# FFN stages of a two-layer trunk: down products moved inside the gate/up blocks, smaller chunks, layer vectors loaded at another place

## The chip, the cores and the metric

The kernel runs on one core of one Trainium2 chip. The metric is the device time of one execution in microseconds (us). Below, TensorE (PE in the profile, with PEld for its weight loads) does the matrix products, VectorE (DVE) and ScalarE (ACT) the elementwise work, GpSimd (POOL) and SyncE (SP) issue transfers (DMAs). SBUF is the working memory, PSUM the memory that matmuls write, here in banks of 512 float32 a partition.

## The reference

The input is 512 tokens of 1024 float32 features; 16 learned tokens are put in front, so T = 528. Two layers follow, each with two feed-forward networks (FFN) around a mixer:

```python
def _swiglu(x, wg, wu, wd):
    return (jax.nn.silu(x @ wg) * (x @ wu)) @ wd

for l in range(DEPTH):                       # DEPTH = 2
    h = _layer_norm(ALPHA * h + 0.5 * _swiglu(h, ffn1_wg[l], ffn1_wu[l], ffn1_wd[l]), ln1_g[l], ln1_b[l])
    m = _mixer(h, ...)                       # convolution branch and RWKV-7 branch
    h = _layer_norm(ALPHA * h + m, ln2_g[l], ln2_b[l])
    h = _layer_norm(ALPHA * h + 0.5 * _swiglu(h, ffn2_wg[l], ffn2_wu[l], ffn2_wd[l]), ln3_g[l], ln3_b[l])
```

wg and wu are 1024 x 2816, wd is 2816 x 1024. The change touches the four FFNs and the loading of the small per-layer vectors, and nothing of the mixer.

## The kernel before

**Products in three parts.** Every float32 operand is held as a high part, rounded to the type float32r, and a low part, the remainder. A product is three matmuls for each 128 rows of the contraction: high x high, high x low, low x high (`mac1`, L204 to L214; the matmul is L210). Features lie on the 128 partitions, tokens along the free dimension, in two halves of n = 264 (256 in the last FFN, which leaves out the 16 learned tokens). KT = 8 is the number of 128-row pieces of the model width, FT = 22 that of the FFN's inner width.

**Splitting weights.** `wunit` (L122) loads a 128 x 1024 piece of weights (512 KB) on SP's queue into a tile `w_raw`, copies it to `w_hi` on ScalarE (L142) and subtracts on VectorE to get `w_lo` (L153). `halve` (L113) does the same for parts of a block; with `dma` set it puts the negated raw weights into `w_lo` on ScalarE (L117) and lets GpSimd issue a DMA that adds the raw weights there (L118), without it VectorE subtracts (L120). The split weights lie in entries of a ring (`entry`, L108), which in an FFN has eight: two, two and four from three pools.

**One FFN** (`ffn`, L427). The inner width is worked off in chunks of 8, 8 and 6 of the 22 pieces (`CHUNKS`, L26). For each chunk come first its gate/up blocks, one for each piece of 128 inner features, and then eight down products, one for each 128 output features, which add their part to `y`. Inner activations are held split, in `hh` and `hl`, eight pieces at a time.

- The first four pieces (`PLAIN`, L27) are *plain* (`up`, L443): gate and up product for each half of the tokens, 2 x 2 x 8 x 3 = 96 matmuls. Then ScalarE's Silu (L457), VectorE's product (L458) and the split into `hh` and `hl` (L105, L106).
- The other 18 are blocks of *seven products* (`up7`, L463), the Strassen-Winograd way for a 2 x 2 cut of weights and tokens: 7 x 4 x 3 = 84 matmuls instead of 96. Their loads (L470) bring gate and up weights (512 KB each) into raw tiles, two from each of two pools by turns. VectorE forms four sums of halves (L476), and five parts are split, three of them through GpSimd's adding DMA. The products go into four banks a, b, c, d of PSUM in the order w1 to a, w6 to b, w7 to c, w5 to d, w2 to a, q4 to c, w3 to d; the last three add to what stands in the bank. Between them VectorE takes the banks' contents over into the tile `ln_sq` (L499), so q4 must wait until c's first content has been read, and w3 the same for d. Two closings (L513) and splits (L105, L106) end a block.
- `make_seven` (L524) builds the token sums t1 to t4 that these blocks use: VectorE first adds high and low part of all tokens into `y` (L534), then forms sums and splits them. t1 overwrites a quarter of the token tile, so it stands behind the last plain block.
- A down product (`down`, L558) loads one piece of wd for the chunk's rows, splits it, and runs 8 (in the last chunk 6) x 3 matmuls for each half; VectorE adds the bank to `y` (L571 for the first chunk, L574 later). For the last chunk it also adds up `ssum` over the features (`add_sum`, L425).

PSUM has six banks for these products (`mm`, L437) and two for the norms' sums. `ln_sq` has two buffers, `w_raw` two in either pool.

**Order.** `stream` (L165) runs the jobs one after another: load and split, products, evacuation. The framework's scheduler then puts each engine's instructions into a fixed order, near that of the program, and may draw loads forward where a buffer is free by its own account; on the chip each engine and queue works in that order, and each instruction waits there for what it needs. The last three jobs (`TAIL`, L41), three downs, are run half by half: all three for the first half of tokens, then the weights ahead for the next stage (`fetch_ahead`, L663) and the first part of the first half's norm (`layer_norm`, L372: mean matmul L380, subtraction L385, square L387, sums L395 to L398, variance matmul L400, reciprocal L402), then all three for the second half. The rest of the norm is run under the start of the next stage.

**Layer vectors.** `layer_vectors` (L313) loads sixteen vectors and time_mix into parts of the tile `ssum` (L321, L323) and conv_w into a tile from the FFN's `ln_sq` buffers (L324), and turns them with TensorE (L327, L328, L336). Both layers' calls are jobs of the very first FFN (L1593), put into the job list at places 4 and 8.

Of the kernel before, what the change touches and what calls it, by code (L numbers as in the profile page):

```python
# [7 lines left out]
F32 = mybir.dt.float32  # L8
# [8 lines left out]
P = 128  # L17
D = 1024
KT = D // P
# [6 lines left out]
CHUNKS = ((0, 8), (8, 16), (16, FT))  # L26
PLAIN = 4  # L27
# [64 lines left out]
class Trunk:  # L92
# [220 lines left out]
    def layer_vectors(self, l, room, mm):  # L313
# [10 lines left out]
        nc.sync.dma_start(out=cwn, in_=self.d["conv_w"][l])  # L324
        vec = lp.tile([P, P], F32, name="vec")
# [101 lines left out]
    def ffn(self, l, which, t0, n, gname, bname, pre, final=False, head=None, extra=()):  # L427
# [7 lines left out]
        tok = [slice(t0 + h * n, t0 + (h + 1) * n) for h in range(2)]  # L435

# [6 lines left out]
        def up(fc, f):  # L443
            cs = slice(fc * P, (fc + 1) * P)

            def load():
                return self.wunit(wg[:, :, cs]), self.wunit(wu[:, :, cs])

            def mac(w, h):
                ps = mm(), mm()  # L450
                return ps, [self.mac1(ps[i][:, :n], w[i], self.x, tok[h], KT) for i in range(2)]

            def evac(h, ps):
                if h == 0:
                    held[fc] = fp.tile([P, 4, 264], F32, name="ln_sq", bufs=2)
                g = held[fc][:, h, :n]
                nc.scalar.activation(g, ps[0][:, :n], AF.Silu)  # L457
                nc.vector.tensor_tensor(g, g, ps[1][:, :n], op=ALU.mult)  # L458
                self.split(g, hh[:, f, tok[h]], hl[:, f, tok[h]])

            return load, mac, evac

        def up7(fc, f):  # L463
            cs = slice(fc * P, (fc + 1) * P)

            def load():
                pool = (self.wp, fp)[fc % 2]
                raw = [pool.tile([P, KT, P], F32, name="w_raw", bufs=2) for _ in range(2)]
                for r, w in zip(raw, (wg, wu)):
                    nc.sync.dma_start(out=r, in_=w[:, :, cs])  # L470
                g1, g2, u1, u2 = (r[:, k:k + KH] for r in raw for k in (0, KH))
                sums = fp.tile([P, 3 * KH, P], F32, name="sums", bufs=1)
                s1 = fp.tile([P, KH, P], F32, name="sum1", bufs=2)
                s2, s3, s4 = (sums[:, i * KH:(i + 1) * KH] for i in range(3))
                for o, a, b in ((s1, u1, u2), (s3, g1, u1), (s2, s1, g1), (s4, s2, g2)):
                    nc.vector.tensor_tensor(o, a, b, op=ALU.add)  # L476
                his, los = zip(*(self.entry() for _ in range(4)))
                lower = slice(0, KH)
                upper = slice(KH, KT)
                whole = slice(0, KT)  # L480
                parts = ((0, whole, raw[0], True), (2, lower, s1, True), (2, upper, u2, True),
                         (1, whole, sums[:, :KT], False), (3, lower, s4, False))
                for e, k, src, dma in parts:
                    self.halve(src, his[e][:, k], los[e][:, k], dma)
                block = lambda e, k: (his[e][:, k], los[e][:, k])
                return [block(0, lower), block(1, lower), block(1, upper), block(2, lower),
                        block(0, upper), block(2, upper), block(3, lower)]

            def mac(w, h):
                if h:  # L490
                    return None, [()]
                w1, w6, w7, w5, w2, q4, w3 = w
                x11, x21, x22, t1, t2, t3, t4 = seven
                run = lambda ps, w, x, first, last: self.together([
                    self.mac1(ps[:, :n], w, x[:2], x[2], KH, x[3], first, last, True)])
                a, b, c, d = (mm() for _ in range(4))
                z = fp.tile([P, 4, 264], F32, name="ln_sq", bufs=2)
                e0, e1, e2, e3 = (z[:, i, :n] for i in range(4))
                add = lambda o, x, y: nc.vector.tensor_tensor(o, x, y[:, :n], op=ALU.add)  # L499
                run(a, w1, x11, True, True)  # L500
                nc.scalar.copy(e0, a[:, :n])
                run(b, w6, t2, True, True)
                add(e0, e0, b)
                run(c, w7, t3, True, True)
                add(e1, e0, c)
                run(d, w5, t1, True, True)
                add(e1, e1, d)
                run(a, w2, x21, False, True)
                nc.scalar.activation(e3, a[:, :n], AF.Silu)
                run(c, q4, t4, False, True)  # L510
                add(e2, e0, c)
                out = [(hh[:, f, t], hl[:, f, t]) for t in tok]
                close = lambda u, g, h: (nc.vector.scalar_tensor_tensor(  # L513
                    u, u, -1.0, g, op0=ALU.mult, op1=ALU.mult), self.split(u, *out[h]))
                close(e2, e3, 0)
                run(d, w3, x22, False, True)
                add(e0, e0, d)
                nc.scalar.activation(e0, e0, AF.Silu)
# [1124 lines left out]
```

## Time and profile before

| | |
|---|---|
| median of 3 runs | 3206.27 us (3200.68 to 3208.75) |
| the profiled execution | 3209.99 us |
| its span, first to last instruction | 3208.3 us |
| mean granted TensorE clock | 0.964 |
| 0 to 447 us | first FFN, with the layer vectors and its norm |
| 447 to 1244 us | mixer of the first layer |
| 1244 to 1646 us | second FFN |
| 1646 to 2046 us | third FFN |
| 2046 to 2816 us | mixer of the second layer |
| 2816 to 3208 us | fourth FFN, norm and store |

The profile is of one execution. Its page gives busy time by engine and the transfers by issuing line with their median time from issue to landing. A view by stretches gives, for each stretch of time, the busy time of each engine and in brackets its number of instructions, then the clock that TensorE was granted (1.00 is full), the mean busy share of the 16 DMA engines and GB/s. Matmuls overlap, so a busy TensorE isn't TensorE at its peak; the count of matmuls in a stretch says more. The view of groups has, behind the bar, busy us and mean ns of one, and behind the second bar the idle time of the engine just before the group, with what ended it. In a timeline a row has start and duration in us, the engine and line, output and input, and in brackets the idle time before it and what ended it. `DVE ln_sq L499` is VectorE's instruction of line 499 that writes `ln_sq`.

### The profile page before, as it was taken

Reading aid. Unit: us, or ns where it says so; the run is one execution under the profiler, and the core shown is the slowest. Engines: PE = TensorE matmul, PEld = TensorE weight load, DVE = VectorE, ACT = ScalarE, POOL = GpSimd, SP = SyncE. Lnnn points to the kernel's source line nnn. Section 1 sums busy time; section 2 is a strip of 40 time slices with the busy share of each in tenths; the row PEclk is TensorE's granted clock in tenths of the full one; section 3 lists DMA queues with packets and bytes.
Section 4 is the critical chain, followed back from the end, with each engine's and each line's share of the span. In section 5 each row is a group of like instructions: output and inputs, shape, how many; then the busy total and the mean of one; then the engine's idle time right before and its main releaser. Section 6 shows DMA issues by size and latency. Waiting matters only on the chain.

```text
span 3208.3 us, 64745 instructions
## 1 busy us (share of the span) xinstructions
PE 3022.6 (94%) x26308; PEld 2878.5 (90%) x26308; DVE 2177.7 (68%) x4471; ACT 1496.6 (47%) x2649; POOL 239.4 (7%) x358
## 2 busy tenths in 40 slices
PE   6999989999999899999989999899999999999997
PEld 5999989989888799999989999899888889989997
DVE  5554667888886677654685646778887748675655
ACT  4453545343554444453554534543444446264543
POOL 1010100000000000010101200000000000011110
PEclk8999999998999999999999999999999999999998
DMA  6566535334455544675636755343353556455761
GB/s 162 129 148 146 120 98 179 97 86 108 119 125 130 174 145 96 147 150 141 152 91 153 165 127 131 123 152 98 89 128 94 140 127 187 120 131 139 180 137 59
DMA packets 607032, 418.77 MB, mean 131 GB/s; under 512 B 90444, under 2 KB 542400, under 8 KB 606734
## 3 DMA queue, kind: packets, MB, share of 16 engines
q1 hardware_dynamic: 564910, 308.49, 33.9%
q0 software_dynamic: 37216, 97.62, 17.3%
q10 hardware_dynamic: 4608, 8.52, 0.7%
q8 instruction: 207, 3.39, 0.4%
q14 instruction: 91, 0.75, 0.1%
HBM read 270.81 MB, written 47.12 MB: 99 GB/s over the span
## 4 chain that ended last, share of the span: by engine, by line
PE 65%; DMA 12%; DVE 9%; issue 9%; ACT 4%; POOL 1%; SPq 0%; ACTq 0%; POOLq 0%; DVEq 0%
PE mm L210 34%; PE mm L229 17%; DMA w_raw<-in_ffn_wu_dram 4%; DMA w_raw<-in_ffn_wd_dram 3%; DMA w_lo<-w_raw 3%; DVE w_lo L153 2%; PE sc L1236 2%; ACT w_hi L142 1%; PE sc L1155 1%; PE tr L1305 1%; PE ch L1330 1%; PE tr L1313 1%; PE ch L1322 1%; POOL w_lo L118 1%; DMA a<-ascr 1%
## 5 line engine op out<-in xcount | busy, mean ns | idle before, releaser
L210 PE MATMUL mm<-xh,w_hi 128*128 128x264 f32 (+1 forms) x1728 | 501.7, 291 | 48.8 <-DVE ln_sq L499 22.6
L210 PE MATMUL mm<-xl,w_hi 128*128 128x264 f32 (+1 forms) x1728 | 499.9, 290 | 0.4
L210 PE MATMUL mm<-xh,w_lo 128*128 128x264 f32 (+1 forms) x1728 | 498.4, 289 | 0.0
L142 ACT CAST w_hi<-w_raw 128x1024 fp32r<-128x1024 f32 (+1 forms) x224 | 227.8, 1018 | 430.7 <-PE mm L210 157.6
L153 DVE TENSOR_TENSOR w_lo<-w_raw,w_hi 128x1024 fp32r<-128x1024 f32 (+2 forms) x280 | 303.5, 1084 | 157.6 <-ACT w_hi L142 151.0
L210 PE MATMUL mm<-hh,w_hi 128*128 128x264 f32 (+1 forms) x1408 | 401.3, 285 | 6.7 <-ACT hh L105 6.6
L210 PE MATMUL mm<-hl,w_hi 128*128 128x264 f32 (+1 forms) x1408 | 400.2, 284 | 2.5 <-DVE hl L106 1.3
L229 PE MATMUL mm<-xh,w_hi 128*128 128x264 f32 x1760 | 393.5, 300 | 7.6 <-DVE kp L858 2.9
L210 PE MATMUL mm<-hh,w_lo 128*128 128x264 f32 (+1 forms) x1408 | 399.1, 283 | 0.0
L229 PE MATMUL mm<-xh,w_lo 128*128 128x264 f32 x1760 | 392.6, 299 | 4.6 <-DMA w_lo<-w_raw 3.3
L229 PE MATMUL mm<-xl,w_hi 128*128 128x264 f32 x1760 | 392.8, 298 | 0.0
L210 PEld LDWEIGHTS mm<-xh,w_hi 128*128 128x128 f32 x1728 | 334.1, 194 | 55.7 <-DVE ln_sq L499 25.1
L984 DVE SCALAR_TENSOR_TENSOR cacc<-cu,cw,cacc 128x528 f32<-128x528 f32 (+1 forms) x480 | 355.6, 752 | 3.4
L210 PEld LDWEIGHTS mm<-xl,w_hi 128*128 128x128 f32 x1728 | 335.7, 194 | 1.8 <-DVE xl L417 1.6
L210 PEld LDWEIGHTS mm<-xh,w_lo 128*128 128x128 f32 x1728 | 335.6, 194 | 0.1
L229 PEld LDWEIGHTS mm<-xh,w_hi 128*128 128x128 f32 x1760 | 287.4, 195 | 16.0 <-DVE kp L858 3.2
L229 PEld LDWEIGHTS mm<-xh,w_lo 128*128 128x128 f32 x1760 | 286.4, 195 | 12.3 <-DMA w_lo<-w_raw 4.1
L229 PEld LDWEIGHTS mm<-xl,w_hi 128*128 128x128 f32 x1760 | 286.5, 194 | 7.6 <-issue 0.2
L210 PEld LDWEIGHTS mm<-hh,w_hi 128*128 128x128 f32 x1408 | 264.9, 188 | 9.7 <-ACT hh L105 9.4
L210 PEld LDWEIGHTS mm<-hl,w_hi 128*128 128x128 f32 x1408 | 265.1, 188 | 6.2 <-DVE hl L106 6.1
L210 PEld LDWEIGHTS mm<-hh,w_lo 128*128 128x128 f32 x1408 | 265.3, 188 | 0.0
L118 POOL DMA_DIRECT2D w_lo<-w_raw x144 | 124.3, 864 | 1319.9 <-ACT w_lo L117 658.4
(356 smaller groups left out, 6715.7 us busy)
## 6 DMA issues: line engine op xcount, KB each, us to landing
w_raw<-in_w_in_dram SPq DMA_DIRECT2D x116, 512.0 KB
w_lo<-w_raw POOLq DMA_DIRECT2D x104, 512.0 KB, 4.9
w_raw<-in_ffn_wg_dram SPq DMA_DIRECT2D x88, 512.0 KB
w_raw<-in_ffn_wu_dram SPq DMA_DIRECT2D x88, 512.0 KB
w_raw<-in_ffn_wd_dram SPq DMA_DIRECT2D x64, 512.0 KB
w_lo<-sum POOLq DMA_DIRECT2D x72, 256.0 KB, 3.9
w_lo<-w_raw POOLq DMA_DIRECT2D x72, 256.0 KB, 5.2
w_raw<-in_ffn_wd_dram SPq DMA_DIRECT2D x32, 384.0 KB
```

Source lines behind the costliest of these rows:

```text
L118: self.nc.gpsimd.dma_start(out=lo.bitcast(F32), in_=x, accum_op=ALU.add)
L142: copy = self.nc.scalar.copy(hi[:, :kt], raw[:, :kt])
L153: sub = self.nc.vector.tensor_tensor(lo[:, k], raw[:, k], hi[:, k].bitcast(F32), op=ALU.subtract)
L210: self.nc.tensor.matmul(pm, a[:, k, :], b[:, xk + k, s], start=first and k == 0 and j == 0, stop=last and k == nk - 1 and j == 2, skip_gro ...
L229: m = nc.tensor.matmul(pm[:, h, :n], a[:, wk + k, :], b[:, xk + k, s:s + n], start=first and k == 0 and j == 0, stop=last and k == nk - 1 ...
L984: tap = nc.vector.scalar_tensor_tensor(y, x, w, y, op0=ALU.mult, op1=ALU.add)
L1155: pairs.append(nc.tensor.matmul(ps[:, e, p * P:(p + 1) * P], FB[p][r, fs], G[r, p, 1, :, cs], start=True, stop=True))
L1236: nc.tensor.matmul(ps[r, i, cs], vt[r, i], x[r, i, cs], start=True, stop=True)
L1305: nc.tensor.matmul(tr[0:C, right(h)], G[:, h // 2, h % 2, 0, cs], sv[:, h, :], start=True, stop=True)
L1313: chain.append(nc.tensor.matmul(tr[C:P, right(h)], G[0:C, h // 2, h % 2, 1, cs], w[0:C, h, :], start=True, stop=True))
L1322: nc.tensor.matmul(ch[HS:P, left(h)], SB[:, c, h, C:2 * C], va[:, h, :], start=True, stop=True, skip_group_check=True)
L1330: chain.append(nc.tensor.matmul(ch[0:C, right(h)], SB[:, c, h, 0:C], va[:, h, :], start=False, stop=True, skip_group_check=True))
```

## The change

- The chunks are of 4, 4, 4, 4, 2 and 4 pieces, and there are five plain blocks instead of four.
- A block of seven products calls `between` behind its fifth product; the order is now w1, w6, w7, w2, w5, then `between`, then q4 and w3. `between` runs one or two *pairs* of down products of the preceding chunk. A pair is two neighbouring outputs: one load of 256 columns (512 KB for four pieces), one split into one entry of the ring, then two products for each half of 4 x 3 matmuls (2 x 3 for the chunk of two pieces), each added to `y`. In the chunk of two pieces two pairs stand in each block. A plain block runs its pair behind its own products.
- The last chunk's eight downs stand behind everything. Their four pairs of weights are prepared ahead; all eight run for the first half, then come `fetch_ahead` and the start of the norm, then all eight for the second half.
- Raw tiles turn over in a fixed order through five buffers, two of the weights' pool and three of the FFN's, for the loads of gate, up and pairs alike (and for the first layer tokens and conv_w). s1 is split by VectorE and not through GpSimd's adding DMA, so two of five parts go that way. The four sums share one tile.
- `y` gets the first half's tokens by two GpSimd DMAs (high part, then low part added) instead of VectorE additions; the token sums are begun behind the third block, and t1 is made behind the fifth.
- The layer vectors' loads are issued behind one block and the transposes behind the next: the first layer's behind the third and fourth block, the second layer's behind the fifth and sixth. conv_w goes to a raw tile.

The core of the diff:

```diff
-CHUNKS = ((0, 8), (8, 16), (16, FT))
-PLAIN = 4
+CHUNKS = ((0, 4), (4, 8), (8, 12), (12, 16), (16, 18), (18, FT))
+PLAIN = 5
...
         nc.sync.dma_start(out=cwn, in_=self.d["conv_w"][l])
+        yield True
         vec = lp.tile([P, P], F32, name="vec")
...
+        def raw():
+            i = raws[0] % 5
+            raws[0] += 1
+            return fp.tile([P, KT, P], F32, name="w_raw", bufs=3) if i > 1 else self.wp.tile(
+                [P, KT, P], F32, name="w_raw", bufs=WB[0])
...
+        def load7(f):
+            cs = slice(f * P, (f + 1) * P)
+            g, u = raw(), raw()
...
+            sums = fp.tile([P, 4, KH, P], F32, name="sums", bufs=1)
...
+            for e, k, src, dma in ((0, whole, g, True), (1, whole, sv[:, :KT], False),
+                                   (2, lower, s1, False), (2, upper, u2, True),
+                                   (3, lower, s4, False)):
+                self.halve(src, his[e][:, k], los[e][:, k], dma)
...
+        def up7(f, between):
+            w1, w6, w7, w5, w2, q4, w3 = load7(f)
...
+            run(a, w1, x11, True, True)
+            nc.scalar.copy(e0, a[:, :n])
+            run(b, w6, t2, True, True)
+            add(e0, e0, b)
+            run(c, w7, t3, True, True)
+            add(e1, e0, c)
+            run(a, w2, x21, False, True)
+            nc.scalar.activation(e3, a[:, :n], AF.Silu)
+            run(d, w5, t1, True, True)
+            add(e1, e1, d)
+            between()
+            run(c, q4, t4, False, True)
+            add(e2, e0, c)
+            close(e2, e3, 0)
+            run(d, w3, x22, False, True)
...
+        def load_pair(a, b, o):
+            hi, lo = self.entry()
+            k = 2 * (b - a)
+            r = raw()[:, :k]
+            nc.sync.dma_start(out=r.rearrange("p (k o) c -> p k (o c)", o=2),
+                              in_=wd[:, a:b, o * P:(o + 2) * P])
+            self.split(r, hi[:, :k], lo[:, :k])
+            return [(hi[:, i:k:2], lo[:, i:k:2]) for i in range(2)]
...
+        def pair(a, b, o):
+            ws = load_pair(a, b, o)
+            for i, w in enumerate(ws):
+                for h in range(2):
+                    pd, products = down(a, b, o + i, w, h)
+                    self.together(products)
+                    add_down(a, b, o + i, h, pd)
...
+        for part, kw in zip(self.x, ({}, {"accum_op": ALU.add})):
+            nc.gpsimd.dma_start(out=y[:, :, tok[0]], in_=part[:, :, tok[0]].bitcast(F32), **kw)
...
+        def later(f):
+            if f == m:
+                join_x(1)
+                next(sums)
+            if f == PLAIN - 1:
+                next(sums)
+            for x in extra[:1]:
+                if next(x, None) is None:
+                    extra.pop(0)
+
+        for i, (a, b) in enumerate(CHUNKS):
+            pairs = [(*CHUNKS[i - 1], o) for o in range(0, KT, 2)] if i else []
+            share = -(-len(pairs) // (b - a))
+
+            def between():
+                for _ in range(min(share, len(pairs))):
+                    pair(*pairs.pop(0))
...
-        self.stream(jobs[m:], TAIL, before,
-                    lambda: self.fetch_ahead(l, which), lambda: next(first))
+        a, b = CHUNKS[-1]
+        if which == 1:
+            self.ring(*self.wy)
+        ws = [w for o in range(0, KT, 2) for w in load_pair(a, b, o)]
+        for h in range(2):
+            if h == 1:
+                self.fetch_ahead(l, which)
+                next(first)
+            for o in range(KT):
...
+                    pd, products = down(a, b, o, ws[o], h)
+                    self.together(products)
+                add_down(a, b, o, h, pd)
```

More of the change, by code (lines that the diff above doesn't have):

```diff
@@ L441, in st @@
             return mm("st", 2)
[L443 to L518, printed above, removed]
-                close(e1, e0, 1)
-                return None, [()]
-            return load, mac, lambda h, ps: None
@@ L580, in ffn @@
-        jobs, held, seven = [], {}, []
-        for a, b in CHUNKS:
-            jobs += [(up if f < PLAIN else up7)(f, f - a) for f in range(a, b)]
-            jobs += [down(a, b, o) for o in range(KT)]
-        sums = make_seven()
-        for i in (PLAIN, PLAIN - 1):
-            jobs.insert(i, (lambda: next(sums), lambda w, h: (None, [()]), lambda h, ps: None))
-        for i, f in extra:
-            jobs.insert(i, (lambda f=f: f(mm), lambda w, h: (None, [()]), lambda h, ps: None))
-        fpool = fp = y = ssum = hh = hl = None
@@ L596, in room @@
             hh, hl = (fp.tile([P, KT, T], F32R, name=x) for x in ("hh", "hl"))
[L597 to L598 removed]
+            return y, ssum, lambda: raw().rearrange("p k c -> p (k c)")
+        def raw():
[3 more added lines that the diff above has]
+                [P, KT, P], F32, name="w_raw", bufs=WB[0])
@@ new lines, in scratch, with inner, load, plain @@
+        def scratch():
+            return fp.tile([P, 4, 264], F32, name="ln_sq", bufs=2)
+        def inner(f, h):
+            return hh[:, f % KT, tok[h]], hl[:, f % KT, tok[h]]
+        def load(f):
+            cs = slice(f * P, (f + 1) * P)
+            return self.wunit(wg[:, :, cs]), self.wunit(wu[:, :, cs])
+        def plain(w, h):
+            ps = mm(), mm()
+            return ps, [self.mac1(ps[i][:, :n], w[i], self.x, tok[h], KT) for i in range(2)]
+        def gate(f, h, ps, z):
+            g = z[:, h, :n]
+            nc.scalar.activation(g, ps[0][:, :n], AF.Silu)
+            nc.vector.tensor_tensor(g, g, ps[1][:, :n], op=ALU.mult)
+            self.split(g, *inner(f, h))
@@ new lines, in up7, with close @@
+        def up7(f, between):
+            w1, w6, w7, w5, w2, q4, w3 = load7(f)
+            x11, x21, x22, t1, t2, t3, t4 = seven
+            run = lambda ps, w, x, first, last: self.together([
+                self.mac1(ps[:, :n], w, x[:2], x[2], KH, x[3], first, last, True)])
+            a, b, c, d = (mm() for _ in range(4))
+            z = scratch()
+            e0, e1, e2, e3 = (z[:, i, :n] for i in range(4))
+            add = lambda o, x, y: nc.vector.tensor_tensor(o, x, y[:, :n], op=ALU.add)
+            def close(u, g, h):
+                nc.vector.scalar_tensor_tensor(u, u, -1.0, g, op0=ALU.mult, op1=ALU.mult)
+                self.split(u, *inner(f, h))
+            run(a, w1, x11, True, True)
[13 more added lines that the diff above has]
+            run(d, w3, x22, False, True)
+            add(e0, e0, d)
+            nc.scalar.activation(e0, e0, AF.Silu)
+            close(e1, e0, 1)
@@ L600, in ffn @@
+        seven = []
         if head is not None:
@@ L605, in ffn @@
         ws = self.ahead
-        ws += [load() for load, mac, evac in jobs[len(ws):m]]
+        ws += [load(f) for f in range(len(ws), m)]
         self.ahead = []
         def heads(h):
-            ps, products = zip(*(jobs[j][1](ws[j], h) for j in range(m)))
+            ps, products = zip(*(plain(ws[f], h) for f in range(m)))
             self.together([x for xs in products for x in xs])
```

144 lines of the change are left out of this document (85 added, 59 removed).

## The prediction

> **What bounds the kernel now.** I read the page, then the stretches by stage, then the groups with their idle time, then timelines inside the feed-forward (FFN) stages. The page:
>
> ```profile
> span 3208.3 us, 64745 instructions
> PE 3022.6 (94%) x26308; PEld 2878.5 (90%) x26308; DVE 2177.7 (68%) x4471; ACT 1496.6 (47%) x2649; POOL 239.4 (7%) x358
> w_lo<-w_raw POOLq DMA_DIRECT2D x104, 512.0 KB, 4.9
> w_lo<-sum POOLq DMA_DIRECT2D x72, 256.0 KB, 3.9
> ```
>
> TensorE is the bound; the question is where it stands still or runs slowly. The stretches by stage (times, matmul counts in brackets, granted clock, DMA share):
>
> ```profile
> core 0: us, PE busy (x) PEld busy (x) DVE busy (x) ACT busy (x) POOL busy (x), PEclk, DMA share, GB/s
> 54.20:77.20 23.00, 0.23 (x3) 0.15 (x2) 10.24 (x17) 4.89 (x10) 2.57 (x3) 0.58 0.58 138
> 77.20:95.00 17.80, 17.80 (x133) 17.74 (x134) 5.70 (x9) 4.92 (x9) 0.00 (x0) 0.87 0.01 2
> 95.00:419.00 324.00, 312.21 (x2509) 308.72 (x2509) 180.41 (x342) 147.52 (x246) 41.28 (x48) 0.99 0.61 141
> 130.00:200.00 70.00, 69.62 (x570) 69.21 (x570) 33.68 (x60) 28.30 (x44) 8.59 (x10) 1.00 0.52 121
> 200.00:240.00 40.00, 34.06 (x266) 32.99 (x265) 25.25 (x49) 24.35 (x44) 9.49 (x11) 0.98 0.87 191
> 234.90:237.90 3.00, 0.27 (x4) 0.05 (x2) 1.10 (x3) 2.19 (x4) 1.22 (x2) 1.00 0.90 181
> 237.90:241.90 4.00, 4.00 (x21) 4.00 (x22) 3.25 (x7) 1.34 (x3) 0.51 (x1) 0.60 1.01 146
> 419.00:447.00 28.00, 19.12 (x128) 17.63 (x127) 25.80 (x43) 13.05 (x20) 0.00 (x0) 0.88 0.15 39
> 1282.00:1615.00 333.00, 316.56 (x2520) 312.86 (x2521) 195.95 (x355) 154.01 (x254) 41.22 (x48) 0.98 0.63 146
> 1340.00:1385.00 45.00, 45.00 (x372) 45.00 (x371) 17.40 (x32) 13.22 (x19) 5.17 (x6) 1.00 0.48 106
> 1385.00:1480.00 95.00, 89.05 (x693) 87.37 (x692) 60.80 (x115) 54.45 (x94) 15.46 (x18) 0.96 0.76 172
> 1646.00:2003.00 357.00, 346.10 (x2796) 342.71 (x2795) 213.84 (x388) 176.65 (x291) 46.43 (x54) 1.00 0.62 139
> 2850.00:3174.00 324.00, 306.44 (x2531) 302.94 (x2530) 185.62 (x348) 148.81 (x252) 43.01 (x50) 0.98 0.63 141
> 3150.00:3170.00 20.00, 20.00 (x170) 20.00 (x171) 7.61 (x18) 0.00 (x0) 0.00 (x0) 1.00 0.01 2
> ```
>
> At 1340 to 1385, pure down products, TensorE never waits: 45/372 = 0.121 us a matmul, my yardstick (0.1176 in the last FFN, 20/170). Against it:
>
> - 54.2 to 95: 40.8 us for 136 matmuls worth 16.5: **24.3 us** lost.
> - The four FFN bodies: 324 - 2509 x 0.121 = 20.4; 333 - 2520 x 0.121 = 28.1; 357 - 2796 x 0.121 = 18.7; 324 - 2531 x 0.1176 = 26.4. Together **93.6 us**.
>
> Inside a body the loss isn't spread evenly. Down products at 130 to 200 lose 70 - 69.0 = 1.0 us at a DMA share of 0.52; blocks of seven products at 200 to 240 lose 40 - 32.2 = 7.8 at 0.87, and 1385 to 1480, which is mostly blocks, 11.1 of 95. What the blocks wait for, from the groups and the VectorE and TensorE timelines:
>
> ```profile
> L476 DVE TENSOR_TENSOR sum<-w_raw 128x512 f32<-128x512 f32 x72 | 49.7, 691 | 164.8 <-DMA w_raw<-in_ffn_wu_dram 164.8
> ```
> ```profile
> 205.30 0.69 DVE L476 TENSOR_TENSOR sum<-w_raw 128x512 f32<-128x512 f32 x1 [7.58 <-DMA w_raw<-in_ffn_wu_dram]
> 205.91 0.42 DVE L499 TENSOR_TENSOR ln_sq<-ln_sq,mm 128x264 f32<-128x264 f32 x1
> 211.44 0.42 DVE L499 TENSOR_TENSOR ln_sq<-ln_sq,mm 128x264 f32<-128x264 f32 x1
> ```
> ```profile
> 211.91 0.39 PE L210 MATMUL mm<-t4h,w_hi 128*128 128x264 f32 x1 [1.69 <-DVE ln_sq L499]
> ```
>
> VectorE runs in order. The sum of the next block's raw weights stands ahead of this block's evacuations (L499); it waits 7.58 us for a load, the evacuations fall behind, and q4, which goes on in bank c, waits 1.69 us for c's earlier evacuation. So the loads are late, VectorE passes the lateness on, and TensorE pays.
>
> **The change, part by part.** *Layer vectors.* Gap and its cause:
>
> ```profile
> L336 PE MATMUL mm<-ident,ln_sq 31*128 31x31 f32 x8 | 1.0, 287 | 22.8 <-DMA ln_sq<-in_conv_w_dram 22.8
> ```
> ```profile
> 54.69 0.48 SPq L321 DMA_DIRECT2D ssum<-in_ln_g_dram  x1
> 63.62 0.57 SPq L323 DMA_DIRECT2D ssum<-in_time_mix_dram  x1
> 69.78 24.88 SPq L324 DMA_DIRECT2D ln_sq<-in_conv_w_dram  x2
> ```
>
> The transposes of conv_w stand in TensorE's queue 22.8 us before their data: conv_w's load needs a ln_sq buffer (two, which the gates and token sums share) and is issued only at 69.78. Changed, conv_w has its own raw buffer (the free second and third of the three in the FFN's pool), and a block stands between the loads and the transposes: 96 matmuls, 11.6 us, plus hoisting. I take all 24.3 us back. The second layer's loads still hold SP's queue for some 9 us (54.69 to 63.62), weight loads behind them; a block with its pair (16.0 us, below) covers that. If it doesn't, at most those 9 us return, so 15 to 24.
>
> *Downs inside the blocks.* A unit is now 84 + 48 = 132 matmuls, 16.0 us. Three raw tiles of five turn over in it: each has 5/3 x 16.0 = 26.6 us from load to load, against 2 x 84 x 0.121 = 20.3 in a run of blocks now. Split weights: 8 entries, 5 a unit, 25.6 us against 20.3. A raw tile's life is its load (wu of 205.30 was waited for 7.58 us) and, if GpSimd reads it, the accumulating transfer (4.9 us), with the VectorE and ScalarE steps between: so 6 us more room is about what was missing. What VectorE must do in a unit, from the groups by shape:
>
> ```profile
> L153 DVE TENSOR_TENSOR w_lo<-w_raw,w_hi 128x1024 fp32r<-128x1024 f32 x192 | 234.7, 1223 | 135.8 <-ACT w_hi L142 133.3
> L499 DVE TENSOR_TENSOR ln_sq<-ln_sq,mm 128x264 f32<-128x264 f32 x270 | 114.7, 425 | 51.1 <-PE mm L210 47.6 <-DVE ln_sq L499 0.5
> L106 DVE TENSOR_TENSOR hl<-ln_sq,hh 128x264 fp32r<-128x264 f32 x132 | 56.1, 429 | 12.6 <-ACT hh L105 10.1
> L120 DVE TENSOR_TENSOR w_lo<-sums,w_hi 128x512 fp32r<-128x512 f32 x72 | 49.6, 689 | 3.6 <-ACT w_hi L115 1.3
> L574 DVE TENSOR_TENSOR y<-y,mm 128x264 f32<-128x264 f32 x96 | 40.5, 427 | 80.3 <-PE mm L210 80.2
> ```
>
> ScalarE loses one activation a block and SP's loads stay as many bytes: at nothing, neither is the bound (ACT 47% of the span). VectorE: four sums at 0.69, a subtraction of 1.22, two of 0.69 (one new: s1 leaves GpSimd, 256 KB of accumulating less a block), five adds of 0.43, two closings and two splits at 0.43 (the closings by the adds' row, same shape), then the pair's 1.22 and four adds at 0.43: 2.76 + 1.22 + 1.38 + 2.15 + 1.72 + 1.22 + 1.72 = 12.2 of 16.0 us, 76%. A block alone has now 8.5 of 10.2, 84%. Per FFN VectorE gains 48 evacuations (20.5 us) and 17 subtractions (11.7 us); at 181 to 214 busy of 324 to 357 they fit. DMA keeps its bytes less the accumulates: 0.61 to 0.63 of a body, now near even instead of 0.5 and 0.87. And q4 and w3, which waited for the evacuations of c and d two products before them, now have the pair's 5.8 us more between.
>
> What remains: at best the 1.5% (1.0/70) that downs lose at 0.52, 20 us of 1338; at worst, if loss grew linearly with the DMA share (1.5% at 0.52, 11.7% at 0.76), 5.8% at 0.62, 77 us, and little is won. A wait on a late buffer has a threshold, so I take the side of the 0.52 row, 34 us: **60 us** back, bounds 17 to 74. New on the way: with eight bank tiles a unit and six banks, a block's a and b reuse the banks that c and d of the block before have just left; b has one product, 1.45 us, for one 0.43 us add.
>
> Part of that is the clock: after the 2.7 us of idleness in the row at 234.9, the next 4 us ran at 0.60 with 21 matmuls, not 33. [...]
>
> *Fifth plain block.* 12 matmuls more in each FFN: 48 x 0.121 = **5.8 us** more, beside nothing. For it the token sums get one block more before their first use; half of them start from a copy by two GpSimd transfers of about 1 MB, behind which nothing is needed for three blocks, so at nothing; without that cover, two landings of 5 us an FFN.
>
> *Tail.* Only the last three downs (18 matmuls a half) ran half by half; now all eight do (12 each): after the first half's mean 96 matmuls cover its norm instead of 54, 5.1 us more. At 419 to 447 TensorE loses 28 - 15.5 = 12.5 us, but VectorE is busy 25.8 of 28 and gets five more adds and sums into that stretch (0.43 each by L574 and by the next row, 4.3 us).
>
> ```profile
> L425 DVE TENSOR_TENSOR ssum<-ssum,y 128x264 f32<-128x264 f32 x36 | 15.5, 431 | 1.0
> ```
>
> Between 0 and 5.1 for each of four tails; I take 2.5, **10 us**.
>
> Sum: 24.3 + 60 + 10 - 5.8 = 88.5. The profiled execution took 3210.0 us (span 3208.3), 3.7 above the median 3206.3: 3121.5 in its terms, **3118** for the median. Own range: steady 17 to 74, vectors 15 to 24, tails 0 to 20, so gains of 26 to 113: 3093 to 3180.
>
> **The rivals.** *The stalls only move* (20%): VectorE still meets unlanded loads in its queue, as at 205.30, and the bodies keep 93.6 us; vectors, tails and the fifth block remain: 24.3 + 10 - 5.8 = 28.5, so 3178. For it: the linear reading above. Against it: the buffers' 26.6 us.
>
> *The vectors' gap stays* (7%), because the loads on SP come just as late: 3118 + 24 = 3142.
>
> *Slower* (7%): the banks become the bound. b of each block waits for d's evacuation; if VectorE is then inside loads' work (a 1.22 and two 0.69, 2.6 us) at each of 68 blocks, TensorE stands 2.5 us each, 170 us instead of 93.6: 3178 + 76 = 3254. It is slower from (93.6 + 28.5)/68 = 1.8 us a block; today's blocks lose 93.6/72 = 1.3. Against it: b needs an add that comes 2.6 us late at every block, and without late loads VectorE has a quarter of the unit free.
>
> *The half clock stays* (4%): it follows neither the gaps nor the waits, and what the clock column costs the bodies, 0.01 x 324 + 0.02 x 333 + 0.02 x 324 = 16 us, doesn't come back: 3134. The 4.0 us at 0.60 right behind the idle 3.0 speak against it.
>
> *No change* (2%): each gain is eaten by part of the slower case.
>
> **How the numbers follow.** The forecast's own case has 60%. The range, 3085 to 3180, takes in that case with its bounds, the gap that stays, the half clock and the stalls that move; its lower end lies 8 us under the case's own, since part of the 20 us that downs lose too may go with the last waits. 0.3% (about 10 us) is what a measurement of this kernel can tell from no change. Faster: 60 + 20 + 7 + 4 = 91%; same 2; slower 7.
>
> **What would show it.** Right: no gap before the conv_w transposes near 54; VectorE's idle time before its first sum, 164.8 us now, under 50; the bodies within 3% of 0.121 us a matmul, with a DMA share of 0.6 to 0.75 throughout. Wrong: xh, w_hi or t2 matmuls released by VectorE's evacuation at each block (banks), or the sum still waiting for loads (rival one), or a tail as long as now.

## The result, and the profile after

The changed kernel took 3113.3 us in the median of 4 runs (3097.5 to 3126.0), the kernel before 3203.5 beside it (3182.5 to 3208.8): a ratio of 0.973, 95% interval 0.966 to 0.980. Four more runs, with which the experiments below are compared, gave 3109.7 (3101.4 to 3112.9) against 3201.6, a ratio of 0.971 (0.969 to 0.973): 92 us less. The forecast was 3118, in a range of 3085 to 3180.

The page of the changed kernel, in the lines that were shown of the one before; its profiled execution took 3097.46 us:

```profile
span 3095.8 us, 64682 instructions
PE 2984.4 (96%) x26356; PEld 2854.5 (92%) x26356; DVE 2276.8 (74%) x4687; ACT 1437.2 (46%) x2551; POOL 178.1 (6%) x286
w_lo<-w_raw POOLq DMA_DIRECT2D x68, 256.0 KB, 3.4
```

TensorE has the 48 matmuls more of the fifth plain block and is busy for 38 us less; the GpSimd transfers of 256 KB that are left land in 3.4 us, not 5.2 (page of before, by the same line). Where the time went shows best in the stretch of an FFN that starts with its first matmul on a token sum t2 and ends with the last: blocks of seven with the downs that stand among them. The stretches of before, one row for each FFN in order of time (time, matmuls in brackets, clock, DMA share, as above):

```profile
93.00:381.50 288.50, 276.71 (x2222) 273.39 (x2221) 161.43 (x304) 140.92 (x238) 41.28 (x48) 0.99 0.64 146
1281.40:1575.50 294.10, 277.98 (x2212) 274.62 (x2211) 170.54 (x310) 143.71 (x241) 41.72 (x49) 0.98 0.66 148
1681.30:1966.50 285.20, 274.30 (x2212) 271.32 (x2210) 163.15 (x304) 142.00 (x238) 42.15 (x49) 0.99 0.67 150
2852.70:3137.70 285.00, 268.16 (x2212) 265.26 (x2211) 168.00 (x310) 141.80 (x240) 42.13 (x49) 0.98 0.68 152
```

And of the changed kernel, with the start of the first FFN (40 to 80), two tails, and two short stretches behind gaps:

```profile
40.00:80.00 40.00, 33.86 (x266) 33.16 (x265) 22.48 (x36) 16.80 (x29) 3.27 (x3) 0.96 0.66 155
93.50:356.70 263.20, 263.20 (x2162) 262.99 (x2161) 181.66 (x346) 122.38 (x210) 26.26 (x31) 1.00 0.60 143
1265.20:1527.40 262.20, 262.20 (x2151) 262.20 (x2150) 181.96 (x342) 124.18 (x208) 26.21 (x31) 1.00 0.60 144
1642.50:1904.70 262.20, 262.20 (x2151) 262.20 (x2151) 182.70 (x342) 124.00 (x208) 26.22 (x31) 1.00 0.60 145
2782.00:3035.90 253.90, 253.90 (x2151) 253.90 (x2150) 179.72 (x342) 123.33 (x208) 26.17 (x31) 1.00 0.61 146
380.90:422.00 41.10, 32.82 (x240) 31.61 (x239) 32.42 (x65) 15.87 (x26) 1.50 (x4) 0.92 0.00 1
1551.10:1586.00 34.90, 27.59 (x192) 26.56 (x191) 29.73 (x51) 14.25 (x20) 0.00 (x0) 0.90 0.30 88
51.69:55.69 4.00, 4.00 (x20) 4.00 (x21) 3.41 (x6) 1.97 (x4) 0.00 (x0) 0.58 1.17 166
410.00:414.00 4.00, 3.96 (x18) 3.96 (x19) 4.00 (x11) 2.13 (x5) 0.00 (x0) 0.50 0.00 0
```

In all four stretches TensorE is busy from end to end at a clock of 1.00: 262.2/2151 = 0.1219 us a matmul, 253.9/2151 = 0.1180 in the last FFN. By that yardstick before lost 288.5 - 2222 x 0.1219 = 17.6, and 24.5, 15.6 and 24.0 in the others, 81.6 together; after loses nothing. What VectorE and TensorE waited for, by groups, after:

```profile
L489 DVE TENSOR_TENSOR sums<-w_raw 128x512 f32<-128x512 f32 x136 | 90.6, 688 | 28.7 <-DMA w_raw<-in_ffn_wu_dram 27.0
L210 PE MATMUL mm<-t4h,w_hi 128*128 128x264 f32 (+1 forms) x272 | 77.3, 284 | 0.0
L210 PE MATMUL mm<-xh,w_hi 128*128 128x264 f32 (+1 forms) x1792 | 513.3, 288 | 22.1 <-ACT xh L417 15.1 <-ACT ln_sq L476 5.4 <-DVE ln_sq L477 0.7
```

The first sum of a block's raw weights (L489) waits 28.7 us for its loads, not 164.8; the matmuls on t4, and those on xh, no longer wait for VectorE's evacuations (now L509). What xh still waits for are the norms (L417), and 5.4 us of gates at the start of the first FFN (L476). The two profiles differ by 112 us, more than the medians, because part of it is no work of the change. Mixer 2, whose code is the same, in before and in after:

```profile
2042.70:2789.00 746.30, 724.26 (x6916) 667.38 (x6916) 559.57 (x1257) 345.97 (x655) 23.12 (x58) 0.96 0.49 134
```
```profile
1968.80:2702.00 733.20, 709.16 (x6914) 652.52 (x6915) 559.77 (x1257) 345.40 (x655) 22.84 (x58) 0.99 0.50 137
```

The same matmuls took 13 us less at a clock of 0.99 in place of 0.96; the second profile of the changed kernel has 0.97 there. So parts of under 10 us are read from stages, not from the time of the whole.

### The profile page after: what moved, and what is told of

Same layout as the page of the kernel before. It is cut to its first block, busy times and chain, and to the rows that moved or that the text cites. A ratio compares the mean times of both kernels' runs of the same rounds, so it can differ in the third digit from the quotient of the medians.

```text
span 3095.8 us, 64682 instructions
## 1 busy us (share of the span) xinstructions
PE 2984.4 (96%) x26356; PEld 2854.5 (92%) x26356; DVE 2276.8 (74%) x4687; ACT 1437.2 (46%) x2551; POOL 178.1 (6%) x286
## 4 chain that ended last, share of the span: by engine, by line
PE 81%; DVE 8%; DMA 5%; ACT 3%; issue 2%; SPq 0%; ACTq 0%; DVEq 0%; POOLq 0%
PE mm L210 50%; PE mm L229 16%; PE sc L1285 2%; PE sc L1204 1%; PE ch L1379 1%; PE tr L1354 1%; PE tr L1362 1%; PE ch L1371 1%; DVE cacc L1033 1%; DVE w_lo L153 1%; DMA w_raw<-in_ffn_wu_dram 1%; DVE ln_rstd L403 1%; DMA w_raw<-in_w_in_dram 1%; ACT w_hi L142 1%; PE sc L957 1%
## 5 line engine op out<-in xcount | busy, mean ns | idle before, releaser
L210 PE MATMUL mm<-xh,w_hi 128*128 128x264 f32 (+1 forms) x1792 | 513.3, 288 | 22.1 <-ACT xh L417 15.1
L210 PE MATMUL mm<-xl,w_hi 128*128 128x264 f32 (+1 forms) x1792 | 512.1, 286 | 0.5 <-DVE xl L418 0.3
L210 PE MATMUL mm<-xh,w_lo 128*128 128x264 f32 (+1 forms) x1792 | 511.6, 286 | 0.5 <-DVE w_lo L153 0.5
L115 ACT CAST w_hi<-sums 128x512 fp32r<-128x512 f32 (+1 forms) x204 | 154.7, 759 | 315.8 <-PE mm L210 205.3
L142 ACT CAST w_hi<-w_raw 128x1024 fp32r<-128x1024 f32 x136 | 142.2, 1048 | 257.9 <-PE mm L229 87.3
L153 DVE TENSOR_TENSOR w_lo<-w_raw,w_hi 128x1024 fp32r<-128x1024 f32 (+1 forms) x192 | 204.0, 1064 | 68.4 <-ACT w_hi L142 62.7
```

The source lines that it names most:

```text
L115: self.nc.scalar.copy(hi, x)
L142: copy = self.nc.scalar.copy(hi[:, :kt], raw[:, :kt])
L153: sub = self.nc.vector.tensor_tensor(lo[:, k], raw[:, k], hi[:, k].bitcast(F32), op=ALU.subtract)
L210: self.nc.tensor.matmul(pm, a[:, k, :], b[:, xk + k, s], start=first and k == 0 and j == 0, stop=last and k == nk - 1 and j == 2, skip_gro ...
```

## The experiments

My theory at the start was the prediction's: pairs of downs inside each block even out what the blocks ask of the loads, and five raw buffers give each load 6 us more. The first rival was that the buffers alone do it. Every kernel ran 4 to 6 times (the layer vectors alone 12 times) beside the kernel before on the same chip. The experiments lie on three chips, so what a kernel gains or loses against another group's is taken from the ratios; their intervals are 95%.

**The changed kernel again.**

> The changed kernel once more, as the yardstick for the other three, which run on the same chip. Both theories: 0.965 to 0.98 of the kernel before (85 to 110 us less). Between two executions of one kernel the unchanged mixer stage alone differed by 13 us in the profiles at hand, so I expect its own median to wander by some 10 us.

3109.7, ratio 0.971 (0.969 to 0.973): as expected, and the yardstick below.

**Pairs ahead of the blocks.** In the changed kernel, for every chunk from the third on:

```diff
+            if a >= PLAIN:
+                while pairs:
+                    pair(*pairs.pop(0))
             for f in range(max(a, m), b):
```

> The changed kernel, but the four pairs of down products of the preceding chunk all stand ahead of the chunk's first block instead of one or two inside each block; buffers, chunks, fifth plain block and layer vectors stay as changed. Theory (interleaving evens out what the blocks ask of the loads): a run of blocks again turns its raw buffers over faster than the loads come, the idle time of VectorE ahead of its first sum goes back from 28 to 100 us or more, and 40 to 75 us of the gain are lost, so about 3155 to 3190. Rival (five raw buffers in place of four do it): at most 15 us lost, so under 3130.

3112.1, ratio 0.972 (0.969 to 0.974). Nothing is lost, and the first sums wait less than with the pairs inside:

```profile
L489 DVE TENSOR_TENSOR sums<-w_raw 128x512 f32<-128x512 f32 x136 | 91.8, 685 | 11.8 <-DMA w_raw<-in_ffn_wu_dram 11.3
```

So my theory falls in its main part: in the changed kernel the place of the pairs is worth nothing that these runs can tell.

**Four raw buffers.** In the changed kernel:

```diff
-            i = raws[0] % 5
+            i = raws[0] % 4
...
-            return fp.tile([P, KT, P], F32, name="w_raw", bufs=3) if i > 1 else self.wp.tile(
+            return fp.tile([P, KT, P], F32, name="w_raw", bufs=2) if i > 1 else self.wp.tile(
...
```

> The changed kernel with four raw weight buffers in rotation in place of five (two in the FFN's pool in place of three). With a unit of 16.0 us and three raw tiles in it, each has 4/3 x 16.0 = 21.3 us from load to load, against 26.6 with five and 20.3 in the kernel before. Theory as predicted (the 6 us of more room are what was missing): the first sum's idle time rises to 100 us or more and 30 to 60 us are lost. Rival (the even demand does it, the buffers have slack): under 10 us lost.

3123.0, ratio 0.976 (0.973 to 0.979): 13 us lost by the medians (the two intervals just touch), between the two expectations. VectorE's waits come back, but TensorE feels few of them (groups, then the worst and the best stretch):

```profile
L489 DVE TENSOR_TENSOR sums<-w_raw 128x512 f32<-128x512 f32 x136 | 91.8, 688 | 119.1 <-DMA w_raw<-in_ffn_wu_dram 118.7
```
```profile
91.10:365.20 274.10, 267.96 (x2162) 266.33 (x2161) 183.63 (x353) 126.94 (x215) 27.09 (x32) 0.99 0.60 145
1648.20:1910.80 262.60, 262.45 (x2152) 262.24 (x2151) 179.52 (x342) 124.03 (x208) 26.22 (x31) 1.00 0.60 145
```

274.1 - 2162 x 0.1219 = 10.6 us lost in the first FFN, 0.3 in the third. 119 us of idle VectorE came with 16 us lost on TensorE, where in before 165 came with 82: idle time of VectorE is a sign, not a price.

**y on VectorE.** In the changed kernel:

```diff
-        for part, kw in zip(self.x, ({}, {"accum_op": ALU.add})):
-            nc.gpsimd.dma_start(out=y[:, :, tok[0]], in_=part[:, :, tok[0]].bitcast(F32), **kw)
...
             if f == m:
+                join_x(0)
                 join_x(1)
```

> The changed kernel, but the first half of the residual y is joined by two VectorE adds where the second half is joined, in place of the two GpSimd transfers of 1 MB behind the norm. Theory (the transfers take 11 us each in the first FFN, and the loads issued beside them are late, 7.8 + 3.1 us lost between 14 and 80 us): the 3.8 us gap near 48 us goes, 3 to 10 us less in all. Rival (VectorE is the nearer bound; two adds of some 2 us more in each FFN delay the token sums): 0 to 10 us more. Predicted: nothing either way.

3102.2, ratio 0.969 (0.967 to 0.972): 7.5 us less, with intervals that overlap. The start of the first FFN tells more; this kernel first, then the changed kernel as it ran beside it:

```profile
40.00:80.00 40.00, 38.22 (x314) 37.52 (x313) 26.78 (x41) 18.53 (x32) 1.87 (x2) 1.00 0.50 137
```
```profile
40.00:80.00 40.00, 30.34 (x227) 29.43 (x227) 20.10 (x27) 14.69 (x25) 3.27 (x3) 0.88 0.64 146
```

87 matmuls more in the same 40 us, 10.6 us by the yardstick (48 and 5.9 us against the first profile of the changed kernel). So the two transfers hold the start of the FFN back.

**The layer vectors alone**, on the kernel before:

```diff
-        nat, tmn, cwn = ssum[:, 0:P], ssum[0:26, P:2 * P], sq()[0:TAPS, 0:D]
+        nat, tmn, cwn = ssum[:, 0:P], ssum[0:26, P:2 * P], self.cwroom()[0:TAPS, 0:D]
...
         nc.sync.dma_start(out=cwn, in_=self.d["conv_w"][l])
+        yield True
...
```

> The kernel before, with the layer vectors alone changed: each layer's loads are issued one to two blocks ahead of its transposes, and conv_w goes into the FFN pool's own raw weight buffer, not into a scratch buffer that gates and token sums share. Theory as predicted: the 22.8 us that the transposes wait go, 15 to 24 us less than the kernel before. Rival (the loads on SP's queue come just as late): 0 to 5 us less.

3182.5, ratio 0.994 (0.992 to 0.996): 20 us less, as the theory has it. Where before had 40.8 us for 136 matmuls, the start of the first FFN now runs through, 259 matmuls (31.6 us by the yardstick) in 31.8:

```profile
40.00:71.80 31.80, 31.03 (x259) 30.47 (x258) 21.26 (x33) 16.22 (x28) 2.75 (x3) 1.00 0.56 133
71.80:362.80 291.00, 278.26 (x2212) 275.26 (x2211) 165.87 (x311) 145.84 (x245) 43.83 (x51) 0.98 0.67 153
```

Its blocks lose as much as ever (291.0 - 269.6 = 21.4 in the first FFN).

**s1 on VectorE alone**, on the kernel before:

```diff
-                parts = ((0, whole, raw[0], True), (2, lower, s1, True), (2, upper, u2, True),
+                parts = ((0, whole, raw[0], True), (2, lower, s1, False), (2, upper, u2, True),
```

> The kernel before, with the split of the sum s1 made by a VectorE subtraction in place of GpSimd's accumulating transfer (72 transfers of 256 KB at 3.9 us go, 72 subtractions at 0.69 us come). The two runs with pairs ahead of the blocks and with four raw buffers have shown that neither the interleaving (0 us) nor the fifth raw buffer (13 us) carries the 50 to 60 us of the bodies. Theory now: transfers are what the blocks are short of, at a DMA share of 0.87, and s1's are part of it: 15 to 45 us less than the kernel before. Rival (long runs of blocks are): within 8 us of the kernel before.

3156.9, ratio 0.984 (0.982 to 0.987): 50 us less for one word, over half of the whole change. The stretches lose 38.1 us in place of 81.6. The best and the worst:

```profile
93.00:367.30 274.30, 271.87 (x2222) 270.10 (x2221) 170.03 (x321) 134.15 (x221) 27.46 (x32) 1.00 0.58 138
2811.80:3091.30 279.50, 268.53 (x2212) 265.94 (x2211) 176.12 (x327) 136.11 (x223) 27.49 (x32) 0.98 0.59 139
```

The likely reason starts from what SP's queue waits for in the kernel before (us in total, times, longest): ahead of its 144 loads for blocks of seven it waited 110 times for a transfer of GpSimd.

```profile
SPq L470 <- DMA w_lo<-w_raw: 780.4, 110, 32.8
```

The timelines of one block show the order: ScalarE makes the lower part of u2, GpSimd's transfer adds u2 to it, and only when that has landed does SP load the raw buffer again. Before:

```profile
200.35 0.86 POOL L118 DMA_DIRECT2D w_lo<-sum  x1 [1.44 <-PE mm L210]
201.54 0.86 POOL L118 DMA_DIRECT2D w_lo<-w_raw  x1 [0.33 <-issue]
208.72 0.37 SPq L470 DMA_DIRECT2D w_raw<-in_ffn_wu_dram  x1
```

With s1 on VectorE:

```profile
200.40 0.87 POOL L118 DMA_DIRECT2D w_lo<-w_raw  x1 [2.11 <-ACT w_lo L117]
204.23 0.37 SPq L470 DMA_DIRECT2D w_raw<-in_ffn_wu_dram  x1
```

From u2's issue to the reload it is 208.72 - 201.54 = 7.2 us behind s1's transfer, and 204.23 - 200.40 = 3.8 without it. In this block the raw buffer is held 3.4 us less. It is a strong case: over all 72 blocks the median from issue to landing of u2's transfer fell by 1.3 us, from 5.2 (page of before) to 3.9:

```profile
w_lo<-w_raw POOLq DMA_DIRECT2D x72, 256.0 KB, 3.9
```

The one word takes away 72 transfers of 256 KB, their place ahead of u2's in GpSimd's queue, and a pass of ScalarE of 0.63 us a block. This run doesn't separate the three.

**s1 on GpSimd again**, in the changed kernel (the same word, the other way):

> The changed kernel, with s1 split by GpSimd's accumulating transfer again, as in the kernel before. If s1's transfers carry the gain: 15 to 45 us more than the changed kernel. If the shorter runs of blocks do: under 8 us more.

3104.3, ratio 0.969 (0.966 to 0.971): nothing lost. Sums wait more, for s1's transfer now, and TensorE not at all:

```profile
L489 DVE TENSOR_TENSOR sums<-w_raw 128x512 f32<-128x512 f32 x136 | 90.7, 688 | 64.4 <-DMA w_lo<-sums 34.8 <-DMA w_raw<-in_ffn_wu_dram 20.1 <-issue 5.7
```
```profile
1266.10:1528.30 262.20, 262.20 (x2152) 262.20 (x2151) 170.87 (x325) 132.07 (x224) 39.77 (x47) 1.00 0.70 159
```

What gains 50 us in the kernel before isn't needed in the changed one: its other parts already cover it. Nor can the bytes alone be what the blocks are short of: at a DMA share of 0.70, above the 0.64 to 0.68 of the kernel before, nothing is lost.

**Chunks of eight.** The run with the pairs ahead, with longer chunks and one down a load for them:

```diff
-CHUNKS = ((0, 4), (4, 8), (8, 12), (12, 16), (16, 18), (18, FT))
+CHUNKS = ((0, 8), (8, 16), (16, 18), (18, FT))
...
```

> The changed kernel with chunks of 8, 8, 2 and 4 and all down products of a chunk behind it, so that up to eight blocks of seven products follow each other, as in the kernel before; the four buffers behind the blocks, s1 on VectorE, the fifth plain block and the tail stay as changed. If the length of a run of blocks carries the gain (eight blocks drain the five raw buffers, four don't): 25 to 55 us more than the changed kernel, about 3135 to 3165, with the idle time ahead of the first sum over 80 us. If s1's transfers do: under 10 us more.

3101.9, ratio 0.968 (0.966 to 0.970): nothing lost, though eight blocks now follow each other. The length of a run of blocks isn't the cause either. The first stretch loses 277.3 - 2234 x 0.1219 = 5.0 us, the other three under 1 us each; the second:

```profile
1258.90:1529.90 271.00, 271.00 (x2224) 270.81 (x2223) 173.89 (x322) 130.43 (x212) 26.21 (x31) 1.00 0.60 142
```

So I formed another theory: one budget. A raw buffer must be loaded, summed, split and passed by GpSimd's last transfer within one turn of the rotation. By it the kernel before misses that by a few microseconds at each block; a shorter hold (s1) or a longer turn (a fifth buffer: in a run of blocks 5/4 x 20.3 = 25.4 us) would each close the gap, and both together would give hardly more than one. The next three runs were to test it.

**Both taken back** in the changed kernel (four raw buffers, s1 on GpSimd):

> The changed kernel with both taken back: four raw weight buffers, and s1 split by GpSimd's accumulating transfer. Alone, the buffer cost 13 us and s1 nothing. Theory (one budget: a raw buffer is held until GpSimd's last transfer from it has landed, and four buffers are enough only when s1's transfer doesn't stand ahead of u2's in GpSimd's queue, or five with it): 35 to 65 us more than the changed kernel, about 3143 to 3173, idle time ahead of the first sum near 165 us. Rival (the two costs are separate and add): 10 to 20 us more, about 3120 to 3128.

3136.0, ratio 0.980 (0.977 to 0.983): 27 us lost by the ratios, with some 12 either way: between the rival's 10 to 20 and the theory's 35 to 65, so that it decides for neither. The first sums wait 182.1 us, more than in the kernel before, but the stretches lose only 19.8 us; the worst:

```profile
91.70:363.90 272.20, 267.48 (x2162) 265.76 (x2161) 172.23 (x337) 134.88 (x232) 40.69 (x48) 0.99 0.70 162
```

With both remedies out, the rest of the change still holds the stretches at 20 us of loss, not 82. This run doesn't tell which part does: four buffers that the downs now share with the blocks, 21.3 us a turn in place of 20.3 with the pairs inside, or the smaller chunks.

**Five raw buffers alone**, on the kernel before:

```diff
-                pool = (self.wp, fp)[fc % 2]
-                raw = [pool.tile([P, KT, P], F32, name="w_raw", bufs=2) for _ in range(2)]
+                raw = []
+                for _ in range(2):
+                    i = raws[0] % 5
+                    raws[0] += 1
+                    pool, bufs = (fp, 3) if i > 1 else (self.wp, 2)
+                    raw.append(pool.tile([P, KT, P], F32, name="w_raw", bufs=bufs))
...
```

> The kernel before, with its blocks of seven taking their raw weight buffers from five in rotation (two of the weights pool, three of the FFN pool) in place of two from each pool by turns; s1 stays with GpSimd. Theory (one budget, either remedy is enough): 30 to 50 us less than the kernel before, near the 47 us that s1 gave. Rival (the buffers are worth 13 us wherever they are put): 5 to 18 us less.

3171.6, ratio 0.991 (0.988 to 0.994): 29 us less (20 to 37), about twice what the same buffer is worth in the changed kernel, and just under the theory's 30 to 50. The stretches lose 45.6 us; the first:

```profile
93.00:373.00 280.00, 273.47 (x2222) 270.55 (x2221) 162.05 (x305) 140.71 (x237) 41.29 (x48) 1.00 0.65 149
```

**Three parts on the kernel before**: s1, the fifth buffer and the layer vectors.

> The kernel before with three parts of the change and no more: s1 on VectorE, five raw buffers in rotation for the blocks, layer vectors loaded ahead with conv_w in a raw buffer. Chunks stay 8, 8 and 6 with their downs behind them, four plain blocks, tail of three. Measured alone, s1 gave 47 and the vectors 21 us. Theory: 65 to 85 us less than the kernel before, 3120 to 3138, so that what is left of the change (chunks of four with pairs, eight halves in the tail, the fifth plain block) is worth 5 to 25. Rival (the pairs inside the blocks and the chunks are needed for the rest): less than 65.

3129.5, ratio 0.976 (0.973 to 0.979): 76 us less. s1 and the vectors alone gave 50 + 20, so beside s1 the fifth buffer adds some 5 us, where alone it gave 29: the two overlap, as one budget has it. But neither is enough, as the theory had it: of the 81.6 us that the stretches lose in the kernel before, s1 alone leaves 38.1, the buffer alone 45.6. What is left for the rest of the change is 0.976 - 0.971, some 17 us, within the 5 to 25 expected. With both (and the vectors), the stretches still lose 20.9 us, in all but the first of them less than with either remedy alone; the last and worst:

```profile
2774.70:3044.70 270.00, 263.73 (x2212) 261.69 (x2211) 172.52 (x322) 134.95 (x222) 27.50 (x32) 1.00 0.61 143
```

**A joined version**: the run with chunks of eight, y's first half on VectorE, four plain blocks.

> The changed kernel with chunks of 8, 8, 2 and 4 whose downs stand behind them, four plain blocks in place of five, and y's first half joined on VectorE. From the parts: 8 us less by chunks_eight and 8 by y_vector (each hardly more than its uncertainty) and 5.8 by the 12 matmuls of the plain block in each FFN: 3085 to 3100 if they add. Rival (the token sums are needed one block earlier and the first block of seven waits for VectorE, some 5 us in each FFN): 3100 to 3115.

3099.9, ratio 0.968 (0.965 to 0.970), against 0.971 (0.969 to 0.973) for the changed kernel: well under the kernel before, and not shown to beat the changed one. The start of its first FFN has no loss left:

```profile
40.00:80.00 40.00, 40.00 (x332) 39.71 (x331) 34.47 (x58) 25.87 (x47) 5.30 (x6) 1.00 0.61 139
```

The rival's wait ahead of the first block of seven isn't there, while the time of the whole sits where both expectations meet; the 5 to 15 us in question are as large as what mixer 2 moves by.

## Why the prediction came out

**Time and range: right.** 3118 against 3113 and 3110. The general mechanism was right too: loads come late, VectorE passes the lateness on, TensorE pays (165 us of waits ahead of the first sums with 82 us lost before, 29 with nothing lost after). But against the sum the bodies gave 22 us more and the start of the first FFN 7 to 14 us less; that these two errors largely cancel is luck, and what the gain was credited to was for the larger part wrong. Most signs that the prediction names for being right came true (the first sums wait 28.7 us, under 50; the DMA share is 0.60), but they come true with the pairs ahead of the blocks as well, so they don't tell which part did it.

**Layer vectors: right, and in part given back to something else.** Predicted 24.3, measured alone 20. In the changed kernel the transposes (now at 70.80 us) wait for nothing. But the start of the first FFN up to its first t2, before and after as stretches, gained less:

```profile
0.00:93.00 93.00, 63.34 (x447) 59.45 (x448) 46.34 (x79) 37.62 (x66) 8.51 (x26) 0.87 0.54 140
```
```profile
0.00:93.50 93.50, 80.26 (x591) 75.81 (x592) 52.20 (x89) 41.72 (x72) 8.37 (x25) 0.98 0.63 167
```

93.0 - 447 x 0.1219 = 38.5 us lost before, 93.5 - 591 x 0.1219 = 21.5 after (99.9 - 590 x 0.1219 = 28.0 in the second profile): 11 to 17 us came back. The difference is the copy of y, which I put at nothing because no result is needed for three blocks. The step failed: what it costs isn't its result but the loads beside it. Timelines of GpSimd and SP in the changed kernel:

```profile
34.34 1.07 POOL L624 DMA_DIRECT2D y<-xh  x1 [30.17 <-PE st L306]
46.46 1.55 POOL L624 DMA_DIRECT2D y<-xl  x1 [11.05 <-DMA y<-xh]
```
```profile
38.90 4.01 SPq L131 DMA_DIRECT2D w_raw<-in_ffn_wg_dram  x1
43.01 3.57 SPq L131 DMA_DIRECT2D w_raw<-in_ffn_wu_dram  x1
```

The second transfer waits 11.05 us for the first, twice the 5 us that I had, and two loads of weights take 4.01 and 3.57 us to issue. ScalarE's cast of the first of them stands ahead of the gates in its order and waits for that load; the gate behind it ends a wait of TensorE of 3.76 us:

```profile
50.30 1.04 ACT L142 CAST w_hi<-w_raw 128x1024 fp32r<-128x1024 f32 x1 [10.95 <-DMA w_raw<-in_ffn_wg_dram]
```

With y on VectorE the same two issues take 0.37 and 2.08 us, the waits of xh's matmuls for gates (L476) come to 1.1 us in the whole run and not to 5.4, and 6 to 11 us come back:

```profile
39.75 0.37 SPq L131 DMA_DIRECT2D w_raw<-in_ffn_wg_dram  x1
42.00 2.08 SPq L131 DMA_DIRECT2D w_raw<-in_ffn_wu_dram  x1
```

**Bodies: the largest term, too small, and laid to the wrong part.** Predicted 60 of 93.6 with bounds of 17 to 74; the stretches alone gained 81.6, above the upper bound. The lower row that I leaned on, 1.0 us lost in 70 at a DMA share of 0.52, isn't a floor: at 0.60, and with s1 on GpSimd at 0.70, the loss is nothing. The threshold that the prediction gives a wait on a late buffer was an estimate, and no run shows where one would lie: in the changed kernel the first sums still wait 28.7 us and the stretches lose nothing, with four raw buffers they wait 119.1 and the stretches lose 16. The failed step is the one on s1: I counted it as a subtraction of 0.69 us more for VectorE and as 256 KB less, and gave its queue no price. Alone it is worth 50 us, most likely since u2's transfer stood behind it and held the raw buffer longer, by 1.3 us in the medians and 3.4 in the block shown. "6 us more room is about what was missing" isn't borne out: in the kernel before, 25.4 us a turn in place of 20.3 leave 45.6 of the 81.6 us, and in the changed kernel, 21.3 in place of 26.6 cost 16 in the stretches. The room there comes from several parts, and the interleaving, after which the change is named, can be taken out at no cost. The clue was on the page of before, in the row that I had not put beside the one of s1 (3.9 us for as many bytes):

```profile
w_lo<-w_raw POOLq DMA_DIRECT2D x72, 256.0 KB, 5.2
```

**Tails: right.** The same stretches before, for the first two of four:

```profile
418.40:458.20 39.80, 29.75 (x199) 27.98 (x198) 31.43 (x58) 16.94 (x28) 1.93 (x4) 0.87 0.11 28
1613.50:1646.00 32.50, 23.97 (x165) 22.83 (x165) 28.61 (x48) 14.69 (x23) 0.00 (x0) 0.84 0.30 82
```

By the yardstick 39.8 - 24.3 = 15.5 against 41.1 - 29.3 = 11.8, 3.7 saved; 12.4 against 11.5, 0.9. The other two give 3.5 and 0.8: 9 us for the predicted 10. The bound named in the prediction fits: VectorE is busy 29.73 of 34.9 us in the second. But neither the gain nor the bound was tested in a run of its own. Nor was the **fifth plain block**: its 48 matmuls are in the page's count and cost 48 x 0.1219 = 5.9 us.

Sum against the two profiles: 81.6 + 17 + 9 - 5.8 = 102 of 112; the rest is mixer 2's 13 us, less some 2.5 by which mixer 1, as little changed, took longer.

**The rivals.** *The stalls only move* and *the banks* fell: in the stretches TensorE waits for nothing, at 136 first sums that still wait 28.7 us. *The half clock stays* fell with 1.00 in all four. The clock column had cost the bodies 16 us by the prediction's sum, and that went together with the gaps: 0.98 to 0.99 in the stretches before, 1.00 after. Elsewhere in the changed kernel gaps remain, and behind three of them the clock was low: behind TensorE's wait of 3.76 us for ScalarE (it ends at 51.69) 0.58 for 4 us, behind 3.48 us at 410 0.50 for 4 us, and behind 2.02 us in the third FFN's tail (it ends at 1952.97) 0.50 from 1953.5 to 1957.5, with two matmuls in it. In the kernel before it was 0.60 for 4 us behind 2.7 us at 234.9. No run was made to test what sets the clock.

**Left open:** which part of the change holds the stretches at 20 us of loss when both remedies are out, and at nothing when they are in, where the kernel before with the same two remedies still loses 21. My guess is that it is the downs' drawing on the same five raw buffers; before, they had the weights pool's two. That wasn't tried, and neither were the new order of the products and the smaller chunks in the kernel before.

## What to carry to other kernels

When a buffer is reloaded too late, list everything that reads it, and look at what stands ahead of the last reader in its queue: a small transfer for something else can hold the buffer (here, most likely, the 256 KB of s1 ahead of u2's: 3.4 us in the block shown, 1.3 in the medians). Price such a hold against one turn of the rotation; a shorter hold and one more buffer work on the same wait, so don't add their gains: here 50 and 29 us apart, some 55 together. And before crediting a large restructuring, make its smallest part alone in the old kernel: here one word gave 50 us in the old kernel, over half of the 92, and the part that gave the change its name could be taken out at no cost.

## What the runs showed that I had not expected

- An issue on SP's queue, 0.37 us in the median of the changed kernel's loads of FFN weights, took 4.01 and 3.57 us while GpSimd's transfers of y were under way, and 0.37 and 2.08 without them. They aren't the only thing that draws an issue out: conv_w's, just ahead of them, took 3.71 us in the one kernel and 3.21 in the other.
- VectorE's idle time ahead of the first sum was 165 us for 82 us lost in one kernel, 119 for 16 in another, 64 for none in a third, 182 for 20 in a fourth: here the idle time of an engine off the critical path doesn't say what it costs.
- Unchanged code moved by 13 us in 746 between two executions, with the granted clock at 0.96 and 0.99.
